# Sums of the attention weights: a column of ones beside V and a third value matmul a step, in place of running additions

## The chip, the cores and the metric

The kernel runs on one core of a Trainium2 chip. Its engines work side by side, each on its own queue of instructions in order: TensorE (PE, matrix products, with its weight loads shown as PEld), VectorE (DVE), ScalarE (ACT), GpSimd (POOL) and SyncE (SP), which here only issues transfers. The metric is the device time of one execution in microseconds, the median of three runs. Every time below comes from those runs or from one profiled execution.

## The reference, cut to what matters

One layer of a decoder trunk over 2048 positions of width 1024, in float32: two groups of heads side by side (a forgetting attention and a spatial gating), a projection, a feed-forward part and a gate. Only the attention is touched by the change. It has 8 heads of width 64 and is causal:

```python
logits = einsum('bhqd,bhkd->bhqk', qb, kh) + cqb[..., :, None] - c[..., None, :]
logits = where(causal, logits, -inf)
probs = softmax(logits, axis=-1)
return einsum('bhqk,bhkd->bhqd', probs, vh)
```

The softmax divides by the sum of the weights over the keys, so each query needs that sum beside its weighted values.

## The kernel before, in words

**Precision.** A float32 operand is cut into a high half (rounded to the matmul's one-pass format, `F32R`) and a low half (the rest), and products are put together from halves. An ordinary product takes three matmuls: high by high, high by low, low by high (`mm3`, L102 to L106).

**Stages.** Phase 1 (to about 568 us) projects x to q, k, v and the gating group and writes q, k and v in halves to the scratch tensors `qS`, `kS`, `vS`. `put_v` (L194) writes V's halves. The attention follows, from about 568 to 1187 us, then the end of the output projection, the feed-forward part and the gate.

**The attention.** A head of query block b (512 queries) takes 4(b+1) steps, one for each tile of 128 keys. The list `heads` (L596) interleaves heads of blocks 0 and 1 first, then all of block 2, then of block 3: 32 heads, 320 steps. In a step, `scores` (L635) makes two matmuls into a PSUM tile `pS` of which there are two (a third, short one adds the causal mask on the diagonal), ACT's exp (L652) turns it into the weights `pr` (keys on partitions, queries along the row), a cast makes the high half of `hl` (L663 on ACT, L661 on DVE or L659 on POOL) and a subtraction the low half (L664, on DVE but for eight steps on POOL). Then L666 adds `pr` to the head's running sum `acc`, on POOL or, by the lists `SUM_DVE` and `HL_POOL`, on DVE; the first step's exp writes `acc` itself. `weigh` (L669) multiplies with V: its stationary tile holds V's high half in 64 columns and the low half in the other 64, so that two matmuls (weights' high half, weights' low half) give all four products, in rows 0 to 63 and 64 to 127 of `pO`.

**Finishing a head.** `finish` (L680) is cut in stages by `yield`. First ACT copies `pO` to `os`. Second, PE transposes `acc` in four pieces, so that DVE can add over the keys within a row (L691) and take the reciprocal. Third, PE transposes `os`, ACT copies the rows of V's low half (L698), DVE adds them to the others (L699) and multiplies with the reciprocals (L704), and SP stores the head (L705). The stages run after the steps 0, 2 and 4 of the next head (`FIN`, L829), for block 0 after 0, 1 and 3. One PSUM tile `pT` serves all these transposes and those of the projection.

**Order.** The loop at L903 writes the order of each engine's queue by hand: in step i it first lets a part of other work go (`mx3`, row maxima of later blocks; `lv`, the late V of block 3; after the weighing, `proj`, the output projection of finished blocks), then the scores of step i + 4 (`LA`), then the weighing of step i, then the stage of `finish` that is due. `fetch` (L843) issues the loads on SP: q for two heads ahead, k and v (`load_kv`, L609) up to six heads ahead in blocks 0 and 1 and one head ahead later, since `KA`, `KS` and `V` hold 4096 keys.

Of the kernel before, what the change touches and what calls it, by code (L numbers as in the profile page):

```python
# [9 lines left out]
F32 = mybir.dt.float32  # L10
F32R = mybir.dt.float32r
AF = mybir.ActivationFunctionType
ALU = mybir.AluOpType
AX = mybir.AxisListType
# [3 lines left out]
P = 128  # L18
S = 2048
D = 1024  # L20
H = 8
HD = 64
AW = 512
FF = 4096
PLE = 256
NT = S // P
TB = 512
NB = S // TB
# [6 lines left out]
def trunk(ctx, tc, x, p, w_in, f_bias, sg_ln_g, sg_ln_b, sg_w, sg_b, att_out_g, sg_out_g,  # L35
# [4 lines left out]
    def pool(stack, name, bufs=1, space=None, side="left"):  # L40
        kw = {} if space is None else {"space": space}
        return stack.enter_context(tc.tile_pool(name=name, bufs=bufs, side=side, reuse_waits="tile", **kw))
# [3 lines left out]
    x, p, out = x[0], p[0, 0], out[0]  # L46
# [3 lines left out]
    dram = ctx.enter_context(tc.tile_pool(name="dram", bufs=1, space=DRAM))  # L50
    qS = dram.tile([NB, H, P + 2, TB], F32, name="qS")
    kS = dram.tile([NB, H, P + 2, TB], F32, name="kS")
    vS = dram.tile([NB, H, P, 4, P], F32, name="vS")
    ysS = dram.tile([NT, P, 4, 2, P], F32, name="ysS")
    attS = dram.tile([S, AW], F32, name="attS")
    hS = dram.tile([S, D], F32, name="hS")
# [137 lines left out]
    def put_v(b, tt, ps, st):  # L194
        evac_split(st, ps, 1.0)
        for hl in range(2):
            sy.dma_start(vS[b, :, :, tt, hl * HD:(hl + 1) * HD].rearrange("h p d -> p h d"),
                         st[:, hl].bitcast(F32).rearrange("p (h d) -> p h d", d=HD))

    class Filler:  # L200
# [328 lines left out]
    aph = ExitStack()  # L529
# [6 lines left out]
    acv = pool(aph, "acv", side="right")  # L536
    small = pool(aph, "small2", 2, side="right")
    pp = pool(aph, "pp", 5, side="right")
    accp = pool(aph, "accp", 2, side="right")
    pS = pool(aph, "pS", 2, PSUM, side="right")  # L540
    pO = pool(aph, "pO", 2, PSUM, side="right")

# [3 lines left out]
    NQ = 3  # L546
    KA = acs.tile([P, KCOLS], F32R, name="KA")
    KS = acs.tile([P, KCOLS], F32R, name="KS")
    V = acv.tile([P, KCOLS // P, P], F32R, name="V")
    QB = [acs.tile([P, TB], F32R, name=f"QB{e}") for e in range(NQ)]  # L550
    QS = [acs.tile([P, TB], F32R, name=f"QS{e}") for e in range(NQ)]
    w_o = [wide[2 * kc:2 * kc + 2] for kc in range(KC)]
# [53 lines left out]
    def dq(k):  # L606
        return sc if k < DQA else sy

    def load_kv(k):  # L609
        b, h = heads[k]  # L610
        bs = slice(int(b == 1), b + 1)
        k0, k1 = slot(k) + bs.start * TB, slot(k) + (b + 1) * TB

        def places(t):
            return t[:, k0:k1].bitcast(F32).rearrange("p (n t) -> p n t", t=TB)

        dq(k).dma_start(places(KS), kS[bs, h, :P].rearrange("n p t -> p n t"))
        dq(k).dma_start(places(KA)[:HD], kS[bs, h, HD:P].rearrange("n p t -> p n t"))
        dq(k).dma_start(V[:, k0 // P:k1 // P].bitcast(F32).rearrange("p (n t) d -> p n t d", t=4),
                     vS[bs, h].rearrange("n p t d -> p n t d"))  # L620

    def load_q(k):
        b, h = heads[k]
# [2 lines left out]
        dq(k).dma_start(QS[e][HD:].bitcast(F32), qS[b, h, :HD])  # L626
        dq(k).dma_start(QB[e][:HD + 2].bitcast(F32), qS[b, h, HD:])

    accs, outs = {}, {}

    HI_DVE = ((), (), (1,), (1, 4, 7, 10))
    SUM_DVE = ((), (), (), (2, 5, 8, 11))
    HL_POOL = ((1,), (), (), ())

    def scores(k, j):  # L635
        b, h = heads[k]
        k0 = slot(k)
        e = qset(k)
        off = max(0, j - 4 * b) * P
        js = slice(k0 + j * P, k0 + (j + 1) * P)  # L640
        ps = pS.tile([P, 512], F32, name="pS")
        pe.matmul(ps[:, off:], KS[:, js], QS[e][:, off:], start=True, stop=False)  # L642
        diag = j >= 4 * b
        by_pe = diag and b < MASKB
        pe.matmul(ps[:, off:], KA[:, js], QB[e][:, off:], start=False, stop=not by_pe)  # L645
        if by_pe:
            pe.matmul(ps[:, off:off + P], dmask_r, ident_r, start=False, stop=True)
        if j == 0:
            accs[k] = accp.tile([P, TB], F32, name="acc")
        acc = accs[k]  # L650
        pr = acc if j == 0 else pp.tile([P, TB], F32, name="pr")
        sc.activation(pr[:, off:], ps[:, off:], AF.Exp, bias=bias_of(b)[:, j, h:h + 1])  # L652
        if diag and not by_pe:
            po.affine_select(out=pr[:, off:off + P], in_=pr[:, off:off + P], pattern=[[1, P]],
                             compare_op=ALU.is_ge, fill=0.0, base=0, channel_multiplier=-1)
        hl = pp.tile([P, 2, TB], F32R, name="hl")
        on_pool = j % 12 in HL_POOL[b]
        if on_pool:
            po.tensor_scalar(hl[:, 0, off:], pr[:, off:], 1.0, 0.0, ALU.mult, ALU.add)  # L659
        elif j % 12 in HI_DVE[b]:  # L660
            ve.tensor_copy(hl[:, 0, off:], pr[:, off:])  # L661
        else:
            sc.copy(hl[:, 0, off:], pr[:, off:])  # L663
        (po if on_pool else ve).tensor_tensor(hl[:, 1, off:], pr[:, off:], hl[:, 0, off:].bitcast(F32), ALU.subtract)  # L664
        if j:
            (ve if on_pool or j % 12 in SUM_DVE[b] else po).tensor_tensor(acc[:, off:], acc[:, off:], pr[:, off:], ALU.add)  # L666
        return hl

    def weigh(k, j, hl):  # L669
        b, h = heads[k]  # L670
        nj = 4 * (b + 1)
        off = max(0, j - 4 * b) * P
        if j == 0:
            outs[k] = pO.tile([P, 512], F32, name="pO")
        o = outs[k]
        vj = V[:, slot(k) // P + j]
        pe.matmul(o[:, off:], vj, hl[:, 0, off:], start=j == 0, stop=False)  # L677
        pe.matmul(o[:, off:], vj, hl[:, 1, off:], start=False, stop=j == nj - 1)  # L678

    def finish(k):  # L680

        b, h = heads[k]
        os = accp.tile([P, TB], F32, name="os", bufs=1)
        sc.copy(os, outs.pop(k))
        acc = accs.pop(k)
        yield
        lt = pT.tile([P, 4, P], F32, name="pT")
        for tt in range(4):
            pe.transpose(lt[:, tt], acc[:, tt * P:(tt + 1) * P], ident)
        l = small.tile([P, 4], F32, name="l")  # L690
        ve.tensor_reduce(l, lt, AX.X, ALU.add)  # L691
        ve.reciprocal(l, l)
        yield
        yt = pT.tile([P, 4, P], F32, name="pT")
        for tt in range(4):
            pe.transpose(yt[:, tt], os[:, tt * P:(tt + 1) * P], ident)
        lo = small.tile([P, 4, HD], F32, name="ylo", bufs=1)
        sc.copy(lo, yt[:, :, HD:])  # L698
        ve.tensor_tensor(lo, yt[:, :, :HD], lo, ALU.add)  # L699
        yo = small.tile([P, 4, HD], F32, name="yo")  # L700
        if k == len(heads) - 1:

            ve.tensor_tensor(tail_yn[0][:, AW - HD:], lo[:, 0], l[:, 0:1].broadcast_to([P, HD]), ALU.mult)
        ve.tensor_tensor(yo, lo, l.unsqueeze(2).broadcast_to([P, 4, HD]), ALU.mult)  # L704
        sy.dma_start(attS[b * TB:(b + 1) * TB, h * HD:(h + 1) * HD].rearrange("(a p) d -> p a d", p=P), yo)  # L705
        yield

# [118 lines left out]
    MASKB = 4  # L826
    PREPT = 54
    GAP = 2
    FIN = (0, 2, 4)  # L829
    LA = 4  # L830
    NPROJ = 5 + 4 * 17 + 6
    tail_yn = []
# [70 lines left out]
    for i, (k, j) in enumerate(steps):  # L903
# [16 lines left out]
            if i - d in WO:  # L920
                f(WO[i - d])
        weigh(k, j, hls.pop((k, j)))
        if late is not None and (j in (0, 1, 3) if b == 0 else j in FIN):
            bb, hh = heads[late[0]]
            if next(late[1], "end") == "end":
                late = None
                if hh == H - 1:
                    proj.gens.append(project(bb))
# [698 lines left out]
```

## Time and profile before

| | us |
|---|---|
| median of three runs (2777.5 to 2779.81) | 2779.11 |
| the profiled execution, device time | 2778.08 |
| its span (first to last instruction) | 2776.3 |
| PE busy (94% of the span) | 2615.6 |
| DVE busy (73%) | 2023.4 |
| ACT busy (48%) | 1342.5 |
| POOL busy (41%) | 1134.3 |

The mean granted clock of PE was 0.984 of full speed. Shares are over the whole span, and the stages differ much: what the attention is bound by is read from its own window. A matmul's recorded duration is its latency, and matmuls overlap, so PE's busy share isn't the share of its peak. Lines of code are given as L664; an entry such as `hl<-pr,hl` names the tiles written and read.

### The profile page before, as it was taken

How to read it: one execution, taken by the hardware profiler on the slowest of the kernel's cores; microseconds unless marked ns; L12 is line 12 of the kernel's file. 1: busy time of each engine (PE TensorE's matmuls, PEld its weight loads, DVE VectorE, ACT ScalarE, POOL GpSimd, SP SyncE). 2: the span in 40 equal slices, each digit the busy share in tenths (PEclk: the TensorE clock that was granted, in tenths of full speed). 3: DMA queues.
4: the chain of work that ended last, by engine and by line, in shares of the span. 5: the costliest groups of instructions: out<-in, count | busy, mean ns of one | idle time of the engine just before them, and what ended most of it. 6: DMA issues, size and time to landing. Idle time of an engine off the chain costs nothing.

```text
span 2776.3 us, 37729 instructions
## 1 busy us (share of the span) xinstructions
PE 2615.6 (94%) x12124; PEld 2139.6 (77%) x12124; DVE 2023.4 (73%) x3316; ACT 1342.5 (48%) x2656; POOL 1134.3 (41%) x949
## 2 busy tenths in 40 slices
PE   8999999898788898987999999999999999999998
PEld 7797878777567676766877878888888888888777
DVE  5546576879999989967888877667977596874333
ACT  6443433357756666644555544455444444452111
POOL 5444443456655645544444322324642171501111
PEclk9999999999999999999999999999999999999999
DMA  5666655587556555364655674447556554673331
GB/s 164 161 168 161 181 147 164 150 212 213 158 141 169 159 167 165 101 198 138 215 203 199 221 254 151 152 144 239 196 172 234 175 168 130 212 251 113 106 107 53
DMA packets 375590, 472.85 MB, mean 170 GB/s; under 512 B 81376, under 2 KB 195424, under 8 KB 375392
## 3 DMA queue, kind: packets, MB, share of 16 engines
q1 hardware_dynamic: 366067, 454.39, 53.3%
q10 hardware_dynamic: 9325, 16.07, 2.1%
q8 instruction: 95, 1.56, 0.2%
q14 instruction: 103, 0.84, 0.1%
HBM read 336.38 MB, written 133.96 MB: 169 GB/s over the span
## 4 chain that ended last, share of the span: by engine, by line
PE 64%; DVE 16%; DMA 7%; issue 5%; POOL 4%; ACT 2%; SPq 1%; DVEq 0%; ACTq 0%; POOLq 0%
PE pf L106 15%; PE pf L104 15%; PE pf L105 15%; DVE hl L664 4%; PE pacc L104 3%; PE pacc L105 3%; PE pacc L106 3%; DMA acc<-hS 2%; DVE mx L172 2%; DMA wraw<-in_w_in_dram 1%; PE pM L169 1%; PE pS L642 1%; POOL lr L1502 1%; PE pO L678 1%; PE pO L677 1%
## 5 line engine op out<-in xcount | busy, mean ns | idle before, releaser
L666 POOL TENSOR_TENSOR acc<-acc,pr 128x512 f32<-128x512 f32 (+3 forms) x240 | 314.9, 1312 | 196.5 <-ACT pr L652 79.1
L1210 POOL TENSOR_TENSOR hq<-hq,hq 128x512 f32<-128x512 f32 x128 | 196.6, 1546 | 336.7 <-ACT hq L1204 304.1
L104 PE MATMUL pf<-B,w1p 128*128 128x512 f32 x752 | 298.4, 397 | 14.6 <-ACT w1p L1004 13.6
L106 PE MATMUL pf<-B,w1p 128*128 128x512 f32 x752 | 296.6, 394 | 2.8 <-DVE w1p L1007 2.8
L105 PE MATMUL pf<-B,w1p 128*128 128x512 f32 x752 | 297.2, 395 | 0.0
L100 POOL TENSOR_TENSOR wsp<-wraw,wsp 128x344 fp32r<-128x344 f32 (+1 forms) x176 | 199.6, 1152 | 194.1 <-ACT wsp L96 187.2
L664 DVE TENSOR_TENSOR hl<-pr,hl 128x512 fp32r<-128x512 f32 (+3 forms) x280 | 259.6, 940 | 6.9 <-ACT hl L663 5.4
L652 ACT ACTIVATE pr<-pS,bias 128x512 f32<-128x512 f32 (+3 forms) x288 | 174.7, 618 | 103.2 <-PE pS L645 43.0
L172 DVE TENSOR_REDUCE mx<-pM 128x1 f32<-128x512 f32 (+3 forms) x288 | 168.6, 593 | 60.4 <-PE pM L169 60.0
L104 PEld LDWEIGHTS pf<-B,w1p 128*128 128x128 f32 x752 | 141.9, 189 | 49.2 <-ACT w1p L1004 14.0
L104 PE MATMUL pf<-R,L 128*128 128x512 f32 x452 | 175.9, 389 | 0.0
L106 PE MATMUL pf<-R,L 128*128 128x512 f32 x452 | 175.8, 389 | 0.0
L105 PE MATMUL pf<-R,L 128*128 128x512 f32 x452 | 175.8, 389 | 0.0
L104 PE MATMUL pacc<-wsp,wide 128*128 128x344 f32 (+1 forms) x480 | 166.3, 347 | 9.5 <-ACT ug L358 6.4
L106 PEld LDWEIGHTS pf<-B,w1p 128*128 128x128 f32 x752 | 141.6, 188 | 37.8 <-DVE w1p L1007 4.8
L105 PEld LDWEIGHTS pf<-B,w1p 128*128 128x128 f32 x752 | 141.7, 188 | 32.0
L106 PE MATMUL pacc<-wsp,wide 128*128 128x344 f32 (+1 forms) x480 | 162.5, 339 | 0.8 <-DVE wide L117 0.8
L105 PE MATMUL pacc<-wsp,wide 128*128 128x344 f32 (+1 forms) x480 | 162.3, 338 | 0.0
L169 PE MATMUL pM<-KM,QM 128*128 128x512 f32 (+2 forms) x320 | 122.8, 385 | 33.9 <-DVE mx L172 19.7
L678 PE MATMUL pO<-hl,V 128*128 128x512 f32 (+1 forms) x320 | 125.2, 392 | 22.6 <-DVE hl L664 20.7
L1007 DVE TENSOR_TENSOR L<-lr,L 128x512 fp32r<-128x512 f32 x113 | 98.0, 867 | 62.8 <-ACT L L1004 62.5
L1007 DVE TENSOR_TENSOR w1p<-ws,w1p 128x512 fp32r<-128x512 f32 (+1 forms) x136 | 118.1, 873 | 34.7 <-ACT w1p L1004 32.1
(452 smaller groups left out, 7388.4 us busy)
## 6 DMA issues: line engine op xcount, KB each, us to landing
hidC<-hq SPq DMA_DIRECT2D x224, 256.0 KB
lr<-hidC SPq DMA_DIRECT2D x224, 256.0 KB
w1raw<-in_w_ff_dram SPq DMA_DIRECT2D x64, 512.0 KB
w1raw<-in_w_ff_dram SPq DMA_DIRECT2D x128, 256.0 KB
wraw<-in_w_in_dram SPq DMA_DIRECT2D x96, 256.0 KB
wraw<-in_w_in_dram SPq DMA_DIRECT2D x88, 172.0 KB
KM<-kS ACTq DMA_DIRECT2D x80, 132.0 KB
jS<-C SPq DMA_DIRECT2D x19, 512.0 KB
```

Source lines behind the costliest of these rows:

```text
L100: e.tensor_tensor(dst[:, 1], src, dst[:, 0].bitcast(F32), ALU.subtract)
L104: pe.matmul(ps, l[0], r[0], start=first, stop=False)
L105: pe.matmul(ps, l[0], r[1], start=False, stop=False)
L106: pe.matmul(ps, l[1], r[0], start=False, stop=last)
L169: pe.matmul(ps[:, :w], q[:, tt * P:(tt + 1) * P], km[:, :w], start=True, stop=True)
L172: ve.tensor_reduce(mx[:, tt, c:c + 1], ps[:, :full], AX.X, ALU.max)
L652: sc.activation(pr[:, off:], ps[:, off:], AF.Exp, bias=bias_of(b)[:, j, h:h + 1])
L664: (po if on_pool else ve).tensor_tensor(hl[:, 1, off:], pr[:, off:], hl[:, 0, off:].bitcast(F32), ALU.subtract)
L666: (ve if on_pool or j % 12 in SUM_DVE[b] else po).tensor_tensor(acc[:, off:], acc[:, off:], pr[:, off:], ALU.add)
L678: pe.matmul(o[:, off:], vj, hl[:, 1, off:], start=False, stop=j == nj - 1)
L1007: (po if lo == "pool" else ve).tensor_tensor(dst[:, 1], src, dst[:, 0].bitcast(F32), ALU.subtract)
L1210: po.tensor_tensor(t, x, y, op)
```

## The change

The stationary tile of V gets 65 columns for each half: 64 of V and one more, which holds 1 beside the high half and 0 beside the low half. A step has three value matmuls, in the order high V by high weights, low V by high weights, high V by low weights, all into the same 65 rows of `pO`. Row 64 then holds the sum of the weights, and rows 0 to 63 the three products added up. (The fourth product, low by low, is no longer in it.)

With this go: `acc` and its 288 additions, its transposes, the reduction over them, ACT's copy of the low rows and the addition of them. `finish` has two stages, after the steps 0 and 2, and takes the reciprocal of column 64 of the transposed output and multiplies straight from PSUM. The eight steps whose halves POOL made go to ACT and DVE. V lies in SBUF as [128, 32, 2, 65], the two columns are set once by POOL, and its load is two transfers, one for each half, with rows of 64 numbers. So that each is one regular pattern, `vS` in memory has the head first, then the position in a tile, then the tile.

```diff
@@ -50,7 +50,7 @@
     dram = ctx.enter_context(tc.tile_pool(name="dram", bufs=1, space=DRAM))
     qS = dram.tile([NB, H, P + 2, TB], F32, name="qS")
     kS = dram.tile([NB, H, P + 2, TB], F32, name="kS")
-    vS = dram.tile([NB, H, P, 4, P], F32, name="vS")
+    vS = dram.tile([H, P, NT, P], F32, name="vS")
     ysS = dram.tile([NT, P, 4, 2, P], F32, name="ysS")
     attS = dram.tile([S, AW], F32, name="attS")
     hS = dram.tile([S, D], F32, name="hS")
@@ -194,7 +194,7 @@
     def put_v(b, tt, ps, st):
         evac_split(st, ps, 1.0)
         for hl in range(2):
-            sy.dma_start(vS[b, :, :, tt, hl * HD:(hl + 1) * HD].rearrange("h p d -> p h d"),
+            sy.dma_start(vS[:, :, 4 * b + tt, hl * HD:(hl + 1) * HD].rearrange("h p d -> p h d"),
                          st[:, hl].bitcast(F32).rearrange("p (h d) -> p h d", d=HD))
 
     class Filler:
@@ -536,7 +536,7 @@
     acv = pool(aph, "acv", side="right")
     small = pool(aph, "small2", 2, side="right")
     pp = pool(aph, "pp", 5, side="right")
-    accp = pool(aph, "accp", 2, side="right")
+    osp = pool(aph, "osp", 1, side="right")
     pS = pool(aph, "pS", 2, PSUM, side="right")
     pO = pool(aph, "pO", 2, PSUM, side="right")
 
@@ -546,7 +546,10 @@
     NQ = 3
     KA = acs.tile([P, KCOLS], F32R, name="KA")
     KS = acs.tile([P, KCOLS], F32R, name="KS")
-    V = acv.tile([P, KCOLS // P, P], F32R, name="V")
+
+    V = acv.tile([P, KCOLS // P, 2, HD + 1], F32R, name="V")
+    for hl in range(2):
+        po.memset(V[:, :, hl, HD:].bitcast(F32), 1.0 - hl)
     QB = [acs.tile([P, TB], F32R, name=f"QB{e}") for e in range(NQ)]
     QS = [acs.tile([P, TB], F32R, name=f"QS{e}") for e in range(NQ)]
     w_o = [wide[2 * kc:2 * kc + 2] for kc in range(KC)]
@@ -616,8 +619,9 @@
 
         dq(k).dma_start(places(KS), kS[bs, h, :P].rearrange("n p t -> p n t"))
         dq(k).dma_start(places(KA)[:HD], kS[bs, h, HD:P].rearrange("n p t -> p n t"))
-        dq(k).dma_start(V[:, k0 // P:k1 // P].bitcast(F32).rearrange("p (n t) d -> p n t d", t=4),
-                     vS[bs, h].rearrange("n p t d -> p n t d"))
+        for hl in range(2):
+            dq(k).dma_start(V[:, k0 // P:k1 // P, hl, :HD].bitcast(F32),
+                            vS[h, :, 4 * bs.start:4 * bs.stop, hl * HD:(hl + 1) * HD])
 
     def load_q(k):
         b, h = heads[k]
@@ -626,11 +630,9 @@
         dq(k).dma_start(QS[e][HD:].bitcast(F32), qS[b, h, :HD])
         dq(k).dma_start(QB[e][:HD + 2].bitcast(F32), qS[b, h, HD:])
 
-    accs, outs = {}, {}
+    outs = {}
 
     HI_DVE = ((), (), (1,), (1, 4, 7, 10))
-    SUM_DVE = ((), (), (), (2, 5, 8, 11))
-    HL_POOL = ((1,), (), (), ())
 
     def scores(k, j):
         b, h = heads[k]
@@ -645,25 +647,17 @@
         pe.matmul(ps[:, off:], KA[:, js], QB[e][:, off:], start=False, stop=not by_pe)
         if by_pe:
             pe.matmul(ps[:, off:off + P], dmask_r, ident_r, start=False, stop=True)
-        if j == 0:
-            accs[k] = accp.tile([P, TB], F32, name="acc")
-        acc = accs[k]
-        pr = acc if j == 0 else pp.tile([P, TB], F32, name="pr")
+        pr = pp.tile([P, TB], F32, name="pr")
         sc.activation(pr[:, off:], ps[:, off:], AF.Exp, bias=bias_of(b)[:, j, h:h + 1])
         if diag and not by_pe:
             po.affine_select(out=pr[:, off:off + P], in_=pr[:, off:off + P], pattern=[[1, P]],
                              compare_op=ALU.is_ge, fill=0.0, base=0, channel_multiplier=-1)
         hl = pp.tile([P, 2, TB], F32R, name="hl")
-        on_pool = j % 12 in HL_POOL[b]
-        if on_pool:
-            po.tensor_scalar(hl[:, 0, off:], pr[:, off:], 1.0, 0.0, ALU.mult, ALU.add)
-        elif j % 12 in HI_DVE[b]:
+        if j % 12 in HI_DVE[b]:
             ve.tensor_copy(hl[:, 0, off:], pr[:, off:])
         else:
             sc.copy(hl[:, 0, off:], pr[:, off:])
-        (po if on_pool else ve).tensor_tensor(hl[:, 1, off:], pr[:, off:], hl[:, 0, off:].bitcast(F32), ALU.subtract)
-        if j:
-            (ve if on_pool or j % 12 in SUM_DVE[b] else po).tensor_tensor(acc[:, off:], acc[:, off:], pr[:, off:], ALU.add)
+        ve.tensor_tensor(hl[:, 1, off:], pr[:, off:], hl[:, 0, off:].bitcast(F32), ALU.subtract)
         return hl
 
     def weigh(k, j, hl):
@@ -674,34 +668,27 @@
             outs[k] = pO.tile([P, 512], F32, name="pO")
         o = outs[k]
         vj = V[:, slot(k) // P + j]
-        pe.matmul(o[:, off:], vj, hl[:, 0, off:], start=j == 0, stop=False)
-        pe.matmul(o[:, off:], vj, hl[:, 1, off:], start=False, stop=j == nj - 1)
+        o = o[:HD + 1, off:]
+        pe.matmul(o, vj[:, 0], hl[:, 0, off:], start=j == 0, stop=False)
+        pe.matmul(o, vj[:, 1], hl[:, 0, off:], start=False, stop=False)
+        pe.matmul(o, vj[:, 0], hl[:, 1, off:], start=False, stop=j == nj - 1)
 
     def finish(k):
 
         b, h = heads[k]
-        os = accp.tile([P, TB], F32, name="os", bufs=1)
-        sc.copy(os, outs.pop(k))
-        acc = accs.pop(k)
-        yield
-        lt = pT.tile([P, 4, P], F32, name="pT")
-        for tt in range(4):
-            pe.transpose(lt[:, tt], acc[:, tt * P:(tt + 1) * P], ident)
-        l = small.tile([P, 4], F32, name="l")
-        ve.tensor_reduce(l, lt, AX.X, ALU.add)
-        ve.reciprocal(l, l)
+        os = osp.tile([HD + 1, TB], F32, name="os")
+        sc.copy(os, outs.pop(k)[:HD + 1])
         yield
         yt = pT.tile([P, 4, P], F32, name="pT")
         for tt in range(4):
-            pe.transpose(yt[:, tt], os[:, tt * P:(tt + 1) * P], ident)
-        lo = small.tile([P, 4, HD], F32, name="ylo", bufs=1)
-        sc.copy(lo, yt[:, :, HD:])
-        ve.tensor_tensor(lo, yt[:, :, :HD], lo, ALU.add)
+            pe.transpose(yt[:, tt, :HD + 1], os[:, tt * P:(tt + 1) * P], ident[:HD + 1, :HD + 1])
+        l = small.tile([P, 4], F32, name="l")
+        ve.reciprocal(l, yt[:, :, HD])
         yo = small.tile([P, 4, HD], F32, name="yo")
         if k == len(heads) - 1:
 
-            ve.tensor_tensor(tail_yn[0][:, AW - HD:], lo[:, 0], l[:, 0:1].broadcast_to([P, HD]), ALU.mult)
-        ve.tensor_tensor(yo, lo, l.unsqueeze(2).broadcast_to([P, 4, HD]), ALU.mult)
+            ve.tensor_tensor(tail_yn[0][:, AW - HD:], yt[:, 0, :HD], l[:, 0:1].broadcast_to([P, HD]), ALU.mult)
+        ve.tensor_tensor(yo, yt[:, :, :HD], l.unsqueeze(2).broadcast_to([P, 4, HD]), ALU.mult)
         sy.dma_start(attS[b * TB:(b + 1) * TB, h * HD:(h + 1) * HD].rearrange("(a p) d -> p a d", p=P), yo)
         yield
 
@@ -826,7 +813,7 @@
     MASKB = 4
     PREPT = 54
     GAP = 2
-    FIN = (0, 2, 4)
+    FIN = (0, 2)
     LA = 4
     NPROJ = 5 + 4 * 17 + 6
     tail_yn = []
@@ -920,7 +907,7 @@
             if i - d in WO:
                 f(WO[i - d])
         weigh(k, j, hls.pop((k, j)))
-        if late is not None and (j in (0, 1, 3) if b == 0 else j in FIN):
+        if late is not None and j in FIN:
             bb, hh = heads[late[0]]
             if next(late[1], "end") == "end":
                 late = None
```

## The prediction

> **What bounds the kernel now.** I read the page first, then the busy time of the engines by stage, the chain of waits of the stage that the change touches, and there the groups by tile shape. The change lives in the attention, from the first value matmul (573 us) to the last (1187 us). The stages in the table of windows are the interleaved heads of query blocks 0 and 1, block 2, and block 3; columns are engine, busy us and count.
>
> ```profile
> span 2776.3 us, 37729 instructions
> ```
>
> ```profile
> 573.00:729.00 156.00, 135.09 (x703) 107.69 (x701) 139.31 (x241) 109.40 (x233) 98.11 (x90) 0.98 0.70 188
> 729.00:949.00 220.00, 187.01 (x855) 145.31 (x854) 207.04 (x363) 138.10 (x278) 126.91 (x108) 0.97 0.59 164
> 949.00:1187.00 238.00, 211.84 (x953) 167.08 (x952) 215.90 (x316) 158.41 (x318) 127.77 (x102) 0.96 0.49 143
> sum 614.00, PE 533.94 PEld 420.08 DVE 562.26 ACT 405.92 POOL 352.79; mean PE 177.98 PEld 140.03 DVE 187.42 ACT 135.31 POOL 117.60
> ```
>
> DVE is busy 562 of 614 us (92%), more than PE in every stage. The chain of waits over the same window has DVE's subtraction for the low half (L664) first:
>
> ```profile
> by line: DVE hl L664 19.7%; issue 9.0%; DVE mx L172 5.4%; PE pS L642 4.7%; PE pO L678 4.6%; PE pO L677 4.5%; PE pS L645 4.5%; PE pW L104 2.9%; PE pW L105 2.9%; PE pW L106 2.8%; ACT pr L652 2.4%; DVE z L761 2.4%; DVE hl L661 2.3%; POOL acc L
> ```
>
> Much of that DVE time is waiting inside instructions. In the order of time, a subtraction that starts beside a POOL addition into the running sum runs until that has ended and its own length is still to come:
>
> ```profile
> 1007.84 1.35 POOL L666 TENSOR_TENSOR acc<-acc,pr 128x512 f32<-128x512 f32 x1 [0.89 <-ACT z L814]
> ...
> 1008.07 1.67 DVE L664 TENSOR_TENSOR hl<-pr,hl 128x512 fp32r<-128x512 f32 x1
> ```
>
> POOL ends at 1009.19, DVE at 1009.74. So POOL's additions, which the chain hardly shows, lengthen DVE, which is the bound. The groups of DVE by shape in the attention, columns: busy us and mean ns, then idle time before:
>
> ```profile
> L664 DVE TENSOR_TENSOR hl<-pr,hl 128x512 fp32r<-128x512 f32 x192 | 213.3, 1120 | 5.4 <-ACT hl L663 4.2
> ...
> L758 DVE SCALAR_TENSOR_TENSOR z<-z,zr,g_post 128x512 f32<-128x512 f32 x24 | 25.6, 1068 | 6.7 <-POOL zr L755 6.7
> L761 DVE TENSOR_TENSOR z<-z,xt 128x512 f32<-128x512 f32 x24 | 24.2, 1007 | 0.0
> L704 DVE TENSOR_TENSOR yo<-ylo,l 128x256 f32<-128x256 f32 x31 | 24.0, 773 | 0.4
> L666 DVE TENSOR_TENSOR acc<-acc,pr 128x512 f32<-128x512 f32 x32 | 22.6, 707 | 1.5 <-POOL acc L666 1.2 <-ACT pr L652 0.3
> L664 DVE TENSOR_TENSOR hl<-acc,hl 128x512 fp32r<-128x512 f32 x32 | 22.5, 705 | 16.2 <-ACT hl L663 15.9
> L691 DVE TENSOR_REDUCE l<-pT 128x4 f32<-128x512 f32 x31 | 21.1, 679 | 5.0 <-PE pT L689 5.0
> ...
> L664 DVE TENSOR_TENSOR hl<-pr,hl 128x384 fp32r<-128x384 f32 x24 | 17.0, 708 | 0.1
> ...
> L699 DVE TENSOR_TENSOR ylo<-pT,ylo 128x256 f32<-128x256 f32 x31 | 12.8, 412 | 0.6 <-ACT ylo L698 0.6
> ...
> L666 DVE TENSOR_TENSOR acc<-acc,pr 128x384 f32<-128x384 f32 x8 | 7.0, 874 | 0.0
> ```
>
> **PE's own need.** A matmul's recorded 0.39 us is its latency. What it takes of PE is the distance to the next start, read where PE waits for nothing:
>
> ```profile
> 574.95 0.34 PE L678 MATMUL pO<-hl,V 128*128 128x384 f32 x1
> 575.13 0.40 PE L642 MATMUL pS<-QS,KS 128*128 128x512 f32 x1
> 575.36 0.39 PE L104 MATMUL pW<-wide,wide 128*128 128x512 f32 x1
> ...
> 576.06 0.28 PE L677 MATMUL pO<-hl,V 128*128 128x256 f32 x1
> 576.18 0.28 PE L678 MATMUL pO<-hl,V 128*128 128x256 f32 x1
> 576.29 0.22 PE L677 MATMUL pO<-hl,V 128*128 128x128 f32 x1
> 576.35 0.28 PE L678 MATMUL pO<-hl,V 128*128 128x128 f32 x1
> ```
>
> That is 0.18 us for 384 columns, 0.23 for 512, 0.12 for 256, 0.06 for 128. The counts:
>
> ```profile
> L677 PE MATMUL pO<-hl,V 128*128 128x512 f32 x224 | 96.1, 429 | 0.6 <-DVE hl L661 0.6
> ...
> L169 PE MATMUL pM<-KM,QM 128*128 128x512 f32 x109 | 46.8, 434 | 19.1 <-DVE mx L172 13.0 <-DVE mx L175 3.7 <-DVE c_all L155 2.3
> ...
> L677 PE MATMUL pO<-hl,V 128*128 128x384 f32 x32 | 11.8, 369 | 0.0
> ```
>
> Four full-row lines of a step (L642, L645, L677, L678) at 224 each, 109 of the maxima, and by the code 576 of the projection (12 row tiles x 2 halves x 8 x 3) and 96 of the late V make 1677 of 512 columns: 386 us. About 137 each of 384 and of 256 columns (four lines x 32, 9 of the maxima) are 25 and 16 us, 265 of 128 columns (128 of the diagonal mask, the rest as before) 16 us, 300 transposes at 0.11 us 33 us. Sum about 476 us, 77% of 614; the count, 2516, agrees with the 2511 of the windows.
>
> **The change, part by part.**
>
> The third matmul, on the path: 224 x 0.23 + 32 x (0.18 + 0.12 + 0.06) = 51.5 + 11.5 = +63 us of PE. A stationary tile of 65 columns isn't in the trace. The nearest row has 8 columns against 128 of the transposes, both f32: the matmul takes the same time, its weight load less.
>
> ```profile
> L146 PEld LDWEIGHTS pM<-ident,mh x32: 82/84/124, 176.2 to 944.5; 128*8 128x8 f32 x32
> L146 PE MATMUL pM<-ident,mh x32: 269/270/415, 176.3 to 944.8; 128*8 128x128 f32 x32
> ```
>
> So I take full rate. Were the f32r stream at 65 columns to fall to the f32 rate of the transposes (0.11 for 128 columns against 0.06), 960 value matmuls would cost nearly double; no row hints at it, and it sits in the slower tail.
>
> The transposes of the sums go: 128 of them; four go out in 0.60 us, so about 0.11 each after the first's 0.27. That is -14 us of PE.
>
> ```profile
> 1105.63 0.60 PE L689 MATMUL pT<-ident,acc 128*128 128x128 f32 x4
> ```
>
> PE after: 476 + 63 - 14 = 525 us. The low half is needed by the third matmul, 0.23 us later than by the second before.
>
> DVE, the bound now: its own 48 additions (two forms above, 22.6 + 7.0, and eight of 256 columns, about 3) -33 us, the reduction L691 -21, the addition L699 -13. Eight subtractions of 384 columns come from POOL: +4 to +6. POOL's 240 additions go, so the waits inside DVE's instructions go: 192 x (1.120 - 0.69, from L664 on `acc`, when POOL has no addition yet, less a little) = 82 us; L704 becomes a PSUM read like L699, 31 x (0.77 - 0.41) = 11; L758 and L761 of the projection, two inputs too, 48 x about 0.32 = 15. Sum 562 - 33 - 21 - 13 + 5 - 82 - 11 - 15 = about 392 us. Should only half of the waits go, 446: in both cases below PE's 525. ACT loses 32 copies of the low rows and gains eight casts, 406 - 12 + 5 = 399. So the bound passes from DVE to PE, whose share of the window decides.
>
> How near does an engine at the bound come to the window's length? DVE now reaches 562/614 = 0.92. Upward, in the feed-forward PE sets the pace nearly alone:
>
> ```profile
> 1300.00:1900.00 600.00, 594.30 (x2579) 477.81 (x2578) 459.39 (x597) 303.50 (x522) 215.71 (x149) 1.00 0.57 191
> ```
>
> 2579 x 0.23 = 593 of 600, 0.99. The attention has short in-order chains through ACT and DVE (two score buffers, scores four steps ahead), so I choose near DVE's share: 0.93. Attention 525/0.93 = 564 us, **-50 us**. The bounds: 525/0.99 = 530 (-84) and, lower than any row of a bound engine, 0.88: 597 (-17).
>
> Finishing a head: two stages instead of three, and the transposes of the output two steps after the copy `os` (step 2, before step 4). The copy stands in ACT's queue behind exps and casts for up to five steps. In the first stage it is close: here the second step's last value matmul (700.02) was ready to be followed by transposes before the copy was done at 701.65.
>
> ```profile
> 700.02 0.40 PE L678 MATMUL pO<-hl,V 128*128 128x512 f32 x1
> ...
> 701.04 0.61 ACT L684 COPY os<-pO 128x512 f32<-128x512 f32 x1
> ```
>
> PE is in order, so scores and values behind them would wait: at most about 1.4 us for each of the 16 heads of this stage, 22 us; at the least nothing. A faster DVE brings PE forward but ACT as well; I take a few us, inside the 0.93. At the end of the attention the shorter chain (no reduction, no copy, no addition) is worth 1 to 2 us; the projection's spatial half already fills PE there. Not counted.
>
> V's loads: one of rows of 2 KB becomes two of pieces of 256 B, 73,728 pieces in all (288 key tiles x 128 x 2) for 9,216 rows. Reads of 256 B aren't in the trace; writes are, those of vS:
>
> ```profile
> DMA packets 2797, 1.03 MB, mean 257 GB/s; under 512 B 2614, under 2 KB 2614, under 8 KB 2796
> ## 3 DMA queue, kind: packets, MB, share of 16 engines
> q1 hardware_dynamic: 2796, 1.02, 104.1%
> ```
>
> In these 4 us (606 to 610) a packet took at most 1.041 x 16 x 4.0/2796 = 24 ns. By that a head of block 3 (4096 pieces) takes 6.1 us of the 16 engines, in a head's 30 us with a DMA share of 0.49: hidden by one head of prefetch. Upper bound: the mean packet of the whole run,
>
> ```profile
> q1 hardware_dynamic: 366067, 454.39, 53.3%
> ```
>
> 0.533 x 16 x 2776.3/366067 = 65 ns, worked out as a rival below. I take 24, the same size. The Trainium skill, "DMA: Bandwidth & Descriptors", Specifications, speaks against the change here: under 512 B an engine does a read-modify-write and misses line rate. The trace's 257 GB/s with nearly all packets under 512 B doesn't bear it out for writes to HBM; for writes to SBUF no row shows it.
>
> SP issues 32 more DMAs at about half a us. Nothing on the path waits for SP's issue itself; the two memsets of the ones and zeros columns run on POOL, which waits 7.48 us for the first exp:
>
> ```profile
> 572.31 0.51 POOL L659 TENSOR_SCALAR hl<-pr 128x384 fp32r<-128x384 f32 x1 [7.48 <-ACT pr L652]
> ```
>
> **Sum.** 2776.3 - 50 = 2726 us of span. The profiled execution took 2778.08, 1.8 over its span, and the median is 1.0 above that: 2729.
>
> **The rivals.**
>
> 1. *PE's stream wasn't waiting for DVE (slower).* PE's idle time is in-order latency: exp to cast to subtraction to value matmul, through two score buffers. Then DVE's relief buys nothing and PE's extra 63 - 14 = 49 us comes on top: 2828. It decides where PE's share stays under 525/614 = 0.855; today's is 0.77. For it: today's low share, and 9% "issue" in the chain. Against: DVE at 92% with L664 leading the chain. 0.11.
>
> 2. *Loads of V in small pieces set the pace.* At 65 ns a piece, eight pairs of heads in the first stage need each 2048 x 65/16 = 8.3 us less the old loads' 1.0 (256 packets) on top of 0.70 x 156/8 = 13.7: 21 us, 168 for the stage; block 2 (16.2 + 10.9) x 8 = 217, block 3 (14.6 + 14.6) x 8 = 233; together 618 against 614: 2783, no gain. It begins to decide, in the first stage, once pieces cost about 45 ns (5.8 - 0.7 + 13.7 = 18.8 us a pair, 150 for the stage). Against it: the 24 ns of the writes; for it: the piece's landing side is SBUF, with rows 520 bytes apart. 0.07.
>
> The Trainium skill's rule on pieces under 512 B, quoted above, would make this rival true if it held for these loads.
>
> 3. *PE fills nearly as in the feed-forward.* 0.97: 541 us, -73, 2706. For it: the weights of the third matmul lie ready and PE's clock, 0.96 to 0.98 with gaps, was 1.00 without. Against: the finishing copies and ACT in the first stage, 109 + 4 in a stage that would shrink towards 135. 0.15.
>
> **How the numbers follow.** The forecast has 0.63, the rivals 0.11, 0.07 and 0.15, and 0.04 is for effects that cancel within 0.2% (5.6 us, what a measurement of this kernel can just tell). Faster: 0.63 + 0.15 + part of rival 2 = 0.82; within 0.2%: 0.05; slower 0.13. The range, 2692 to 2772, runs from 0.98 of PE's need to a gain of 7 us; it leaves out rival 1, most of rival 2 and little else.
>
> **What would show it.** Right: DVE's L664 near 0.69 us in the mean and DVE's busy time in the attention under 450 us; three value matmuls 0.23 us apart; the attention about 565 us long; PE's waits on `hl` nearly gone. Wrong: L664 still above 1 us (then POOL wasn't the cause); PE waiting for V or KS by DMA (rival 2); the attention at 600 us or more with DVE under 70% (rival 1); transposes of `os` waiting for ACT's copy by more than 20 us in all.

## The result, and the profile after

The changed kernel takes 2717.71 us in the median (2708.95 to 2721.12), the kernel before beside it 2778.31: a ratio of 0.978, 95% interval 0.9766 to 0.9796, so 57 to 65 us less. The forecast was 2729, 50 us less. The profiled execution took 2715.74 us.

```profile
span 2714.0 us, 37423 instructions
```

The lines of the changed kernel have moved: scores L644 and L647, exp L651, casts L657 and L659, the subtraction L660, the value matmuls L672 to L674, the finish L680 to L691. Here is the table of stages again, each window from the first value matmul of its stage to that of the next (columns as before: PE, PEld, DVE, ACT and POOL busy, granted clock, DMA share, GB/s):

```profile
572.00:715.00 143.00, 134.26 (x741) 103.58 (x741) 92.99 (x216) 110.82 (x231) 0.36 (x3) 0.96 0.86 209
715.00:910.00 195.00, 187.15 (x911) 141.18 (x910) 146.56 (x338) 134.37 (x263) 9.34 (x18) 0.98 0.76 182
910.00:1129.00 219.00, 218.31 (x1052) 163.25 (x1051) 130.00 (x262) 159.82 (x312) 13.98 (x23) 1.00 0.65 155
sum 557.00, PE 539.72 PEld 408.00 DVE 369.55 ACT 405.01 POOL 23.68; mean PE 179.91 PEld 136.00 DVE 123.18 ACT 135.00 POOL 7.89
```

The attention takes 557 us where it took 614: 13 us less in the first stage, 25 in block 2, 19 in block 3. DVE went from 562 to 370 us busy, POOL from 353 to 24, and PE is recorded busy for 218.3 of 219 us in block 3, at full clock. What is left of the 62 us of span, some 5, lies outside the attention, most of it behind. From the start of the last value matmul to the end it is 1589.1 us before and 1584.8 after. That isn't a gain of the change that can be told: in the profiles of the runs below, one each, this stretch takes 1585.4 to 1591.7 us with the new finish and 1586.5 to 1593.4 with the old one. The groups of DVE by shape:

```profile
L660 DVE TENSOR_TENSOR hl<-pr,hl 128x512 fp32r<-128x512 f32 x224 | 152.7, 688 | 87.6 <-ACT hl L659 71.3 <-PE pM L106 7.5 <-PE pW L106 2.5
...
L745 DVE SCALAR_TENSOR_TENSOR z<-z,zr,g_post 128x512 f32<-128x512 f32 x24 | 17.6, 749 | 8.3 <-POOL zr L742 8.3
...
L748 DVE TENSOR_TENSOR z<-z,xt 128x512 f32<-128x512 f32 x24 | 16.4, 683 | 0.0
...
L691 DVE TENSOR_TENSOR yo<-pT,l 128x256 f32<-128x256 f32 x31 | 13.0, 420 | 0.4
```

The subtraction is at 0.688 us in the mean, from 1.120, and DVE is now idle for 87.6 us before it, 71.3 of them for ACT's cast, where before it was 5.4. The projection's two operations, which the change doesn't touch, went from 1.07 and 1.01 to 0.75 and 0.68 us. In the order of time, the value matmuls of block 3 and the next scores:

```profile
1000.30 0.39 PE L672 MATMUL pO<-hl,V 128*65 128x512 f32 x1
1000.53 0.39 PE L673 MATMUL pO<-hl,V 128*65 128x512 f32 x1
1000.76 0.39 PE L674 MATMUL pO<-hl,V 128*65 128x512 f32 x1
1000.99 0.39 PE L644 MATMUL pS<-QS,KS 128*128 128x512 f32 x1
```

They start 0.23 us apart, with 65 columns as with 128. PE's waits in the whole attention (total us, times, longest) were led by DVE before:

```profile
PE pO L678 <- DVE hl L664: 20.7, 24, 3.6
PE pM L169 <- DVE mx L172: 14.0, 12, 2.6
```

And after:

```profile
PE pM L169 <- DMA KM<-kS: 6.8, 3, 4.0
PE pS L644 <- ACT pr L651: 6.1, 6, 2.3
PE pS L647 <- DMA QB<-qS: 1.1, 1, 1.1
PE pM L169 <- DVE mx L172: 0.7, 3, 0.3
...
PE pO L674 <- DVE hl L660: 0.5, 1, 0.5
```

The waits for DVE are nearly gone, and a load leads the list.

### The profile page after: what moved, and what is told of

Read it like the earlier page. It is cut to its first block, busy times and chain, and to the rows that moved or that the text cites. A ratio compares the mean times of both kernels' runs of the same rounds, so it can differ in the third digit from the quotient of the medians.

```text
span 2714.0 us, 37423 instructions
## 1 busy us (share of the span) xinstructions
PE 2620.9 (97%) x12316; PEld 2127.5 (78%) x12316; DVE 1822.2 (67%) x3212; ACT 1342.5 (49%) x2632; POOL 806.6 (30%) x695
## 4 chain that ended last, share of the span: by engine, by line
PE 46%; DMA 4%; DVE 4%; POOL 2%; issue 2%; ACT 1%; SPq 0%; DVEq 0%; POOLq 0%; ACTq 0%
PE pf L106 15%; PE pf L104 15%; PE pf L105 15%; DMA acc<-hS 2%; POOL lr L1489 1%; DMA w1raw<-in_w_ff_dram 1%; DVE lr L1486 1%; DVE lr L1488 1%; DVE w1p L994 0%; DMA px<-hS 0%; DMA T<-hS 0%; DMA B<-jS 0%; DVE ws L1170 0%; POOL hq L1197 0%; DMA cS<-px 0%
## 5 line engine op out<-in xcount | busy, mean ns | idle before, releaser
L660 DVE TENSOR_TENSOR hl<-pr,hl 128x512 fp32r<-128x512 f32 (+1 forms) x320 | 191.9, 608 | 104.6 <-ACT hl L659 87.9
L651 ACT ACTIVATE pr<-pS,bias 128x512 f32<-128x512 f32 (+1 forms) x320 | 196.6, 622 | 108.8 <-PE pS L647 66.2
L659 ACT CAST hl<-pr 128x512 fp32r<-128x512 f32 (+3 forms) x272 | 146.5, 549 | 8.6 <-DMA vS<-hl 2.2
L991 ACT CAST L<-lr 128x512 fp32r<-128x512 f32 x113 | 70.3, 622 | 150.1 <-PE pf L105 120.1
L991 ACT CAST w1p<-w1raw 128x512 fp32r<-128x512 f32 (+1 forms) x123 | 73.4, 598 | 128.7 <-PE pf L105 121.9
```

The source lines that it names most:

```text
L660: ve.tensor_tensor(hl[:, 1, off:], pr[:, off:], hl[:, 0, off:].bitcast(F32), ALU.subtract)
L991: sc.copy(dst[:, 0], src)
```

## The experiments

**POOL's additions taken out of the kernel before.** The theory was that they lengthen DVE's instructions and that DVE sets the pace; the rival, that they are hidden.

```diff
-        if j:
-            (ve if on_pool or j % 12 in SUM_DVE[b] else po).tensor_tensor(acc[:, off:], acc[:, off:], pr[:, off:], ALU.add)
+        if j and (on_pool or j % 12 in SUM_DVE[b]):
+            ve.tensor_tensor(acc[:, off:], acc[:, off:], pr[:, off:], ALU.add)
...
-        ve.reciprocal(l, l)
+        ve.tensor_scalar(l, l, 1.0, None, ALU.add)
```

> The kernel before without POOL's 240 additions into the running sums (so the sums are not computed; 1 is added to what is there in place of the reciprocal). Everything DVE and PE are given stays. Theory (POOL's additions hold up DVE's two-input operations, and DVE is the bound): the mean of L664 on 512 columns falls from 1.12 to about 0.7 us, DVE's busy time in the attention from 562 to about 455 us, the attention from 614 to 510 to 535 us, the time to 2676 to 2700. Rival (POOL's additions were hidden, DVE's own additions and reductions were what counted): 2770 to 2780.

Measured: 2681.66 us, ratio 0.968 (0.9658 to 0.9702), 82 to 95 us less. In this kernel, the subtraction's group and the sum over the attention's stages:

```profile
L664 DVE TENSOR_TENSOR hl<-pr,hl 128x512 fp32r<-128x512 f32 x192 | 130.5, 687 | 17.6 <-ACT hl L663 16.3
```

```profile
sum 518.00, PE 503.16 PEld 409.58 DVE 417.01 ACT 403.43 POOL 39.13; mean PE 167.72 PEld 136.53 DVE 139.00 ACT 134.48 POOL 13.04
```

The theory holds: without one DVE instruction less, DVE's busy time falls from 562 to 417 us and the attention from 614 to 518. The rival is out. This is more than the whole change brings, since PE has no third matmul here.

It isn't only instructions with two inputs that get shorter. DVE's casts have one, and fall as well; its reductions, which read PSUM, stay as they were. First the kernel before, then this one:

```profile
L661 DVE CAST hl<-pr 128x512 fp32r<-128x512 f32 x40 | 29.4, 736 | 1.4 <-ACT pr L652 1.3
L172 DVE TENSOR_REDUCE mx<-pM 128x1 f32<-128x512 f32 x101 | 67.5, 677 | 2.3 <-PE pM L169 2.2
```

```profile
L661 DVE CAST hl<-pr 128x512 fp32r<-128x512 f32 x40 | 16.9, 423 | 5.2 <-ACT pr L652 5.1
L172 DVE TENSOR_REDUCE mx<-pM 128x1 f32<-128x512 f32 x100 | 67.5, 683 | 6.2 <-PE pM L169 5.8
```

**The third matmul put into the kernel before.**

```diff
         pe.matmul(o[:, off:], vj, hl[:, 0, off:], start=j == 0, stop=False)
+        pe.matmul(o[:, off:], vj, hl[:, 0, off:], start=False, stop=False)
         pe.matmul(o[:, off:], vj, hl[:, 1, off:], start=False, stop=j == nj - 1)
```

> The kernel before with a third value matmul a step, the first one repeated into the same sum (so the weighted values come out doubled). Nothing else changes. Theory (PE had room: 476 us of need in 614): the need becomes 539, still under DVE's 562, so the attention grows by 0 to 25 us, time 2778 to 2804. Rival (PE's waits are in-order latency, so its work adds in full): +63 us, 2841.

Measured: 2799.99 us, ratio 1.0107 (1.009 to 1.0124), 25 to 34 us more.

```profile
sum 636.00, PE 585.34 PEld 473.40 DVE 559.85 ACT 414.25 POOL 341.53; mean PE 195.11 PEld 157.80 DVE 186.62 ACT 138.08 POOL 113.84
```

The rival is out. The time lies inside the theory's 2778 to 2804, near its upper end, and the attention grew by 22 us, inside its 0 to 25; beside the kernel before in the same round (2772.75) the growth of 25 to 34 is at or just over what it allowed. DVE's busy time is the same 560 us, and 63 us of PE work came on top. So PE's work was hidden for the most part, but not wholly, though DVE was the longer engine.

**One of the three matmuls taken out of the changed kernel.**

```diff
         pe.matmul(o, vj[:, 0], hl[:, 0, off:], start=j == 0, stop=False)
-        pe.matmul(o, vj[:, 1], hl[:, 0, off:], start=False, stop=False)
         pe.matmul(o, vj[:, 0], hl[:, 1, off:], start=False, stop=j == nj - 1)
```

> The changed kernel without the value matmul of low V by high weights (that product is left out). Theory (PE is the bound after the change): its need falls by 63 us to 462, the attention from 557 to about 495 to 515 us, the time from 2718 to 2656 to 2676. Rival (the attention is now set by ACT's chain or by loads): 2700 to 2718.

Measured: 2676.29 us, at the upper end of the theory's range and far below the rival's, ratio to the kernel before 0.9653 (0.9637 to 0.9668) where the changed kernel has 0.9781: by the ratios 36 us less. Its stages:

```profile
571.00:713.00 142.00, 129.54 (x657) 91.87 (x655) 97.15 (x226) 106.55 (x226) 0.35 (x3) 0.96 0.85 206
713.00:887.00 174.00, 167.95 (x810) 126.98 (x810) 140.91 (x329) 133.50 (x270) 8.45 (x18) 0.99 1.02 230
887.00:1081.00 194.00, 192.41 (x925) 146.36 (x924) 127.99 (x260) 156.60 (x311) 13.61 (x23) 1.00 0.62 155
```

Block 2 lost 21 us and block 3 lost 25; the matmuls taken out there need, at 0.23, 0.18, 0.12 and 0.06 us, 8 x (9 x 0.23 + 0.36) = 19 and 8 x (13 x 0.23 + 0.36) = 27. So there PE is the bound: the two stages lost 46 us for 46 of need, read from one profile of each kernel. The first stage lost 1 us for 16 of PE work: something else sets it.

**One-input copies in place of POOL's additions, in the kernel before.** Is it POOL's second input that holds DVE, or any POOL work?

```diff
+        elif j:
+            for _ in range(2):
+                po.tensor_scalar(acc[:, off:], pr[:, off:], 1.0, 0.0, ALU.mult, ALU.add)
```

> The kernel before with each of POOL's 240 additions replaced by two one-input copies of the same tile into the running sum (so the sums are not computed), about 1.2 us of POOL in place of 1.3 to 1.5. Theory A (any POOL work on the same memory holds DVE up): time as before, 2765 to 2780, L664 near 1.1 us. Theory B (only additions with two inputs hold DVE up): as without POOL's additions, 2676 to 2710, L664 near 0.7 us with POOL as busy as before.

Measured: 2729.41 us, ratio 0.9836 (0.9813 to 0.9859): between the theories, so neither holds as put. POOL's copies and DVE's subtraction by shape:

```profile
L669 POOL TENSOR_SCALAR acc<-pr 128x512 f32<-128x512 f32 x320 | 267.3, 835 | 110.9 <-ACT pr L652 25.2 <-DVE hl L664 19.1 <-DVE acc L666 17.0
```

```profile
L664 DVE TENSOR_TENSOR hl<-pr,hl 128x512 fp32r<-128x512 f32 x192 | 163.4, 859 | 6.2 <-ACT hl L663 5.1
```

POOL is more busy than with additions (two copies of 0.84 us in place of one addition of 1.51 in the mean), and the subtraction still takes 0.86 us, against 0.69 alone and 1.12 beside additions. One-input POOL work holds DVE up too, but a subtraction seems to lose one short copy rather than one long addition; that last reading is argued from the means, not shown.

The run also bears on another way in which POOL could slow the kernel, one that no run takes apart: it reads `pr` and so keeps that tile from the next exp. ACT's exp waited for POOL like this, in the kernel before and then with the copies:

```profile
ACT pr L652 <- POOL acc L666: 7.5, 9, 1.5
```

```profile
ACT pr L652 <- POOL acc L669: 15.3, 19, 2.1
```

The copies keep the tile longer, and the kernel is 45 us faster, so this isn't the main cause.

**POOL's additions kept in the changed kernel**, into a tile that nobody reads.

```diff
+        if j and j % 12 not in SUM_DVE[b]:
+            po.tensor_tensor(accx[:, off:], accx[:, off:], pr[:, off:], ALU.add)
         return hl
```

> The changed kernel with POOL's 240 additions of the weights kept, into one more tile that nobody reads. Theory (the additions hold DVE up, and PE is the bound without them): the mean of L660 goes back above 0.9 us, DVE's busy time in the attention from 370 to 450 to 490 us, near enough to PE's need of 516 to 525 us that the attention grows by 8 to 38 us; time 2726 to 2756. Rival (POOL's additions cost nothing once PE is the bound, since DVE has room): 2713 to 2722.

Measured: 2766.61 us, ratio 0.9963 (0.9949 to 0.9978). Of the gain of 61 us some 10 are left: the additions alone cost 50. The theory has the cause right and the size too small (8 to 38), and the rival's zero is far off.

```profile
L663 DVE TENSOR_TENSOR hl<-pr,hl 128x512 fp32r<-128x512 f32 x224 | 244.9, 1107 | 36.9 <-ACT hl L662 32.8 <-PE pM L106 2.1 <-PE pS L650 0.8
```

```profile
sum 608.00, PE 556.10 PEld 409.68 DVE 513.94 ACT 405.70 POOL 323.22; mean PE 185.37 PEld 136.56 DVE 171.31 ACT 135.23 POOL 107.74
```

The subtraction is back at 1.107 us. DVE is busy 514 of 608 us (0.85), less than the share at which it was the bound before (0.92), and PE's need of 525 is 0.86 of it. Neither engine is full, and yet the attention is 51 us longer than without the additions. PE waits for DVE again:

```profile
PE pM L169 <- DVE mx L172: 17.3, 14, 3.4
...
PE pO L679 <- DVE hl L663: 8.4, 11, 3.5
PE pT L771 <- DVE yn L715: 5.4, 3, 3.2
```

So DVE holds PE up in places though it isn't full on average, and the longer engine divided by 0.93 (565 us) doesn't give the length of 608. No run takes these 43 us further apart.

**What sets the first stage.** Three edits of the changed kernel, alone and together. The first puts V's low half ahead of the high half, so that both and the column of ones lie side by side and one load of 512-byte pieces brings them. The second moves casts of blocks 0 and 1 from ACT to DVE. The third has both.

```diff
-        for hl in range(2):
-            dq(k).dma_start(V[:, k0 // P:k1 // P, hl, :HD].bitcast(F32),
-                            vS[h, :, 4 * bs.start:4 * bs.stop, hl * HD:(hl + 1) * HD])
+        dq(k).dma_start(V[:, k0 // P:k1 // P, :2 * HD].bitcast(F32),
+                        vS[h, :, 4 * bs.start:4 * bs.stop])
...
-    HI_DVE = ((), (), (1,), (1, 4, 7, 10))
+    HI_DVE = ((1,), (1, 3, 5), (1,), (1, 4, 7, 10))
```

> The changed kernel with V's low half ahead of its high half in each key tile, so that both halves lie side by side (128 numbers, 512 bytes) before the one column of ones, and one load brings them; the matmul of low V takes 64 columns and writes 64 rows. Half as many pieces and one issue less for each head. Theory (blocks 0 and 1 are now set by loads that come late, the rest by PE): the first stage shortens from 143 to 132 to 139 us, the others stay; time 2706 to 2715 where the changed kernel has 2718. Rival (ACT's exps and casts set the first stage): 2716 to 2720.

> The changed kernel with 32 of the casts for the high halves of blocks 0 and 1 moved from ACT to DVE (steps 1 of block 0; 1, 3 and 5 of block 1). ACT's work in the first stage falls by about 18 us, DVE's grows by about 13. Theory (loads set the first stage): 2714 to 2722. Rival (ACT sets it): the first stage shortens by 5 to 14 us, 2704 to 2713.

> The two last edits together. If loads alone count: as with the first of them. If each takes part of the first stage's waits: 2698 to 2710. PE's need in that stage, 122 us, is the floor: the stage isn't shorter than about 130 us, the time not below 2705 by this alone if the other stages stay.

Measured: 2715.50 us (ratio 0.9779, 0.9759 to 0.9799), 2712.96 (0.978, 0.9758 to 0.9801) and 2722.17 (0.9808, 0.9789 to 0.9827), where the changed kernel has 0.9781. None is told from it by the ratios. By the times alone the first lies between its two ranges, the second in the rival's (2704 to 2713) and the third above all of its own; with ratios so near, these are no verdicts. The first stage of the three, in this order:

```profile
574.00:717.00 143.00, 133.73 (x742) 102.92 (x743) 93.75 (x220) 111.67 (x233) 0.36 (x3) 0.98 0.85 215
```

```profile
571.00:711.00 140.00, 132.52 (x742) 101.34 (x742) 101.02 (x248) 97.90 (x198) 0.35 (x3) 0.99 0.87 214
```

```profile
572.00:719.00 147.00, 134.10 (x747) 103.56 (x746) 103.83 (x256) 101.10 (x203) 0.36 (x3) 0.97 0.83 215
```

So neither relieving ACT by 13 us nor halving the pieces of V's loads shortens the stage by more than 3 us, and one profile of each doesn't tell 3 us: with both edits the stage took 147. The DMA share stays at 0.83 to 0.87 in all three, which led to the next run: loads taken out that have nothing to do with V.

```diff
+        po.memset(QS[e][:HD].bitcast(F32), 0.0)
...
-        sy.dma_start(wo_raw[n], w_out[kc * P:(kc + 1) * P, hs])
+        po.memset(wo_raw[n], 0.01)
...
-        dq(k).dma_start(QS[e][:HD].bitcast(F32), qS[b, h, :HD])
```

> The changed kernel with some 20 us of the 16 transfer engines' work taken out of the first stage: the load of q's high half beside low k is left out (that product is left out), and the 16 tiles of the output projection's weights are set to a constant by POOL instead of loaded. Theory (the first stage, 143 us long with a DMA share of 0.88, is set by loads): it shortens to 130 to 137 us, the other stages stay; time 2702 to 2712. Rival (it is set by the short steps' own chain through ACT and DVE): 140 to 144 us, 2714 to 2720.

Measured: 2702.88 us, ratio 0.9739 (0.9719 to 0.9759).

```profile
574.00:709.00 135.00, 129.76 (x739) 101.72 (x739) 94.84 (x222) 112.53 (x232) 7.65 (x17) 0.99 0.77 185
```

The first stage is 8 us shorter, with the same PE work and ACT as busy as before, and both the stage and the time lie in the theory's ranges: loads take part in setting it. PE's own waits for loads in this stage didn't shrink (2.0 us in the changed kernel, 3.0 here), but its waits for the exp did (6.1 to 1.7). One place in the changed kernel's trace shows how a load gets there through ACT:

```profile
702.26 0.62 ACT L580 CAST wide<-xt 128x512 fp32r<-128x512 f32 x1 [2.10 <-DMA xt<-in_w_out_dram]
```

```profile
704.04 0.80 PE L644 MATMUL pS<-QS,KS 128*128 128x512 f32 x1 [2.33 <-ACT pr L651]
...
705.16 0.63 PE L674 MATMUL pO<-hl,V 128*65 128x512 f32 x1
705.59 0.52 PE L644 MATMUL pS<-QS,KS 128*128 128x384 f32 x1
```

ACT's cast of the projection's weights waits 2.10 us for their load, the exps stand behind it in ACT's queue, and PE waits 2.33 us for an exp. Then the granted clock of PE is 0.50 for the next 2 us, and a matmul of 512 columns takes 0.43 us to the next start instead of 0.23. These weights are among the loads left out of this run, and there the granted clock of the stage is 0.99 in place of 0.96. How many of the 8 us go this way, and what the other loads do, isn't shown; V's pieces, when half of them were saved, weren't it.

**A version with two matmuls again.** The sum needs one column, V's halves need 128, and the tile has 128. Giving up the low half of one channel of 64 makes room:

```diff
-        pe.matmul(o, vj[:, 0], hl[:, 0, off:], start=j == 0, stop=False)
-        pe.matmul(o, vj[:, 1], hl[:, 0, off:], start=False, stop=False)
-        pe.matmul(o, vj[:, 0], hl[:, 1, off:], start=False, stop=j == nj - 1)
+        pe.matmul(o, vj, hl[:, 0, off:], start=j == 0, stop=False)
+        pe.matmul(o, vj, hl[:, 1, off:], start=False, stop=j == nj - 1)
...
+        sc.copy(ylo[:, :, :HD - 1], yt[:, :, HD + 1:])
+        ve.tensor_tensor(yo, yt[:, :, :HD], ylo, ALU.add)
```

> The changed kernel with two value matmuls again: one stationary tile of 128 columns holds V's high half in 64, the ones in one, and the low half of the first 63 channels in the rest (the low half of V's last channel is left out). A head's finish gets back ACT's copy of the low rows and one DVE addition. Theory (PE is the bound in blocks 2 and 3): its need falls by about 60 us, ACT's grows by 12 and DVE's by 13, which have room; the attention 495 to 515 us, time 2660 to 2685. Rival (the longer finish in ACT's queue stops PE at the two-stage finish): 2690 to 2715.

Measured: 2690.54 us, ratio 0.970 (0.9681 to 0.9718), better than the changed kernel by some 22 us and 5 us above the range expected. Block 3 and block 2 by stage:

```profile
713.00:900.00 187.00, 174.02 (x816) 141.09 (x815) 145.90 (x343) 136.18 (x278) 8.56 (x18) 0.96 0.81 192
900.00:1096.00 196.00, 194.89 (x921) 159.90 (x919) 130.03 (x268) 158.17 (x318) 15.02 (x23) 1.00 0.70 171
```

Block 3 gained 23 us, near the 27 of PE's need. Block 2 gained 8 where the run with a matmul less had gained 21. The maxima's loads of k now hold PE more (the whole attention; before the edit 6.8):

```profile
PE pM L169 <- DMA KM<-kS: 14.9, 6, 4.2
```

Of these, 12.3 us fall in block 2, against 4.1 in the run with a matmul less. So what PE's relief uncovers in block 2 is for the most part a load; for the finish in ACT's queue PE doesn't wait there. The other 5 of the 13 us aren't traced.

## Why the prediction was right, point by point

**The bound was DVE, lengthened by POOL's additions.** Shown: taking out the additions alone gave 82 to 95 us, putting them back into the changed kernel took 50 of 61, and the subtraction's mean followed each time (1.12, 0.69, 1.11). The forecast of 0.69 us for the subtraction came out at 0.688, and that of 392 us for DVE's busy time at 370: the sum has no term for the casts (14 us, at 512 and 384 columns) and for the shorter subtractions, which POOL had held up too. The Trainium skill, "GPSIMD Engine Reference", Specifications, says that POOL shares its interfaces to SBUF with VectorE, with contention for DVE instructions that have two SBUF inputs or run in a two-port mode; the trace agrees for two inputs, and puts 0.43 us on each subtraction of 512 columns here. DVE's own 67 us of removed work (additions, reduction, addition of the low rows) were taken off its busy time, but no run shows what they alone are worth: with PE at the bound, DVE has 187 us to spare.

**The third matmul, 63 us of PE.** The need was right: the matmuls start 0.23 us apart, and taking one out gives blocks 2 and 3 back what it needs. That 65 columns cost as much as 128 was taken from a row with 8 columns, and holds. Its weights load faster (135 ns in the median, 188 with 128 columns), which is hidden:

```profile
L672 PEld LDWEIGHTS pO<-hl,V x320: 133/135/228, 571.9 to 1128.9; 128*65 128x65 f32 x160
```

**PE's share of the window: the term that was mis-sized.** I chose 0.93 and got 525/557 = 0.943, so 564 became 557: 7 of the 11 us by which the forecast was off. But it is a mean of unlike stages. An estimate of PE's need by stage, from the matmuls counted in each window of the changed kernel at the distances above, is 125 of 143 us, 181 of 195 and 217 of 219: 0.87, 0.93 and 0.99. Block 3 is at PE's own pace; the first stage is set by other things, loads among them. That one share came so near for all three is in part luck. The rule behind it, that the longer engine over a share gives the length, failed in two runs: with additions kept, the longer need is 525 and the window 608; with a third matmul in the old kernel it is DVE's 560, which over its share of before (0.92) gives 609, and the window is 636. In both, two engines are each near 0.85 to 0.88 of the window, and the window is longer than either; that they wait for each other is read from PE's waits in the first of them. In the changed kernel it didn't matter, since DVE fell to 0.66. By the prediction's own bound, "Should only half of the waits go, 446: in both cases below PE's 525", half the waits were harmless; after the run with additions kept, which has DVE at 514, I wouldn't say so.

**The range.** Its lower end, 2692, is called 0.98 of PE's need, but 525/0.98 = 536 us of attention would give 2701; 2692 belongs to 0.996. The result lies above both.

**The end of the attention**, "worth 1 to 2 us, not counted". The two profiles differ by 4 us behind the last value matmul, less than that stretch scatters by from run to run, so the rest of the 11 us has no cause that a run shows.

**Finishing in two stages.** Bounded at 22 us, taken as a few. PE's waits for the copy (what its engines waited for ahead of the operations on `os`):

```profile
  ACT os L680: 2.1, 4
```

2.1 us in four waits. The step holds.

**V's loads in small pieces.** The number of packets rose as worked out and the queue's share with it:

```profile
q1 hardware_dynamic: 430179, 454.39, 56.9%
```

0.569 x 16 x 2714.0 less 0.533 x 16 x 2776.3 is 1032 us of engine time more. If the 9,216 old rows cost the mean of 65 ns each, they freed 599, and a piece costs (1032 + 599)/73,728 = 22 ns, an estimate near the 24 read from the writes. So rival 2 fell at the price. But small pieces aren't free. In the run with V's halves side by side the queue moved the same bytes in

```profile
q1 hardware_dynamic: 377971, 454.39, 55.1%
```

which is 0.551 x 16 x 2716.8 = 23,951 us, 757 less than the 24,708 of the changed kernel, though the time of the kernel stayed. The Trainium skill's rule on pieces under 512 B ("DMA: Bandwidth & Descriptors", Specifications: they miss line rate) has no price, so by itself it didn't make rival 2 true; these 757 us agree with its direction. The prediction's 257 GB/s for the writes had no larger pieces beside it and couldn't tell. Still the DMA share of the first stage went from 0.70 to 0.86, and there loads do take part in the pace.

**The rivals.** Rival 1 (PE's work adds in full) fell with the third matmul in the old kernel: 25 to 34 us and not 63 (the transposes stay in that run), though a part of it is true. Rival 3 (0.97) lies below what block 3 reached and above the other stages.

## What to carry to other kernels

Work on an engine off the critical path can be the cause of the path: look for instructions of the bound engine whose mean is far above their shortest, and at what else was running on the same memory beside the long ones. Trading that work for PE work pays where PE has room, but price it by stage, since each stage may have another bound behind the first. And when two engines each need some 0.85 of a stage, as in two runs here, the sum by the longer one can be too short.

## What was not expected of the hardware

One-input POOL copies also hold DVE's two-input operations up (0.86 against 0.69 us in the mean), less than POOL's additions (1.12). POOL's additions hold DVE's one-input casts up too (0.74 against 0.42 us), but not its reductions from PSUM (0.68 us in both). And 240 POOL additions cost 50 us of the whole while no engine was busy more than 0.92 of the attention: with them PE was busy 556 of 608 us by its records, which count latency, and by its need of 525 only 0.86.
